# Gate and up projections by Strassen's seven block products in place of eight, with weight sums from accumulating transfers

## The chip, the cores and the metric

The kernel runs on one core of one Trainium2 chip. The metric is the device time of one execution in microseconds, lower is better. The engines named below are PE (TensorE, the matrix engine; PEld is its loading of stationary operands), DVE (VectorE), ACT (ScalarE), POOL (GpSimd) and SP (SyncE, which here only starts transfers).

## The reference

One decoder layer on 512 tokens of width 1024 in float32: a SwiGLU feed-forward layer (FFN1), two causal token mixers side by side, a second SwiGLU layer (FFN2), and a last norm. The change touches the two feed-forward layers only (D_FF is 2816).

```python
def rmsnorm(x, g):
    xf = x.astype(f32)
    y = xf * lax.rsqrt(jnp.mean(xf * xf, axis=-1, keepdims=True) + EPS)
    return (y * g.astype(f32)).astype(x.dtype)

def swiglu(x, w_gate, w_up, w_down):
    return (jax.nn.silu(x @ w_gate) * (x @ w_up)) @ w_down
...
    x = x + 0.5 * swiglu(rmsnorm(x, norm_ffn1), ffn1_gate, ffn1_up, ffn1_down)
    h = rmsnorm(x, norm_mix)
...
    x = x + 0.5 * swiglu(rmsnorm(x, norm_ffn2), ffn2_gate, ffn2_up, ffn2_down)
    return x
```

## The kernel before

Everything is kept transposed: features on the 128 partitions, the 512 tokens along the free dimension. X holds the residual stream as eight tiles of 128x512. Each fp32 product is made of three fast ones (`mac`): an operand is split into a high part, rounded to the fast type, and a low part, the rest, and PE computes high·high, high·low and low·high. So every operand needs a cast on ACT (the high part) and a subtraction on DVE (the low part).

The weights come in an order written out in the list `stream`. `fetch` starts the transfer of a tile of 128x1024 (512 KB) from SP into one of three `raw` buffers, `split` makes the parts `whi` (ACT, L192) and `wlo` (DVE, L193), two buffers each, and `weights` hands a tile out and sees to it that the next one is split and the ones behind it are under way.

A feed-forward layer is `ffn(i, tail)`, with i = 0 for FFN1 and i = 2 for FFN2. For each of 22 column tiles m of the hidden layer it makes the gate and the up product, each over 8 tiles of the contraction: 48 matmuls of 128x512. The norm's factor per token is not applied to the input but behind the product: XN holds X times the gain, split in two, and `factors` computes the row R (tile `rrow`) from the sum of squares. That row is there only behind tile m = 1 (`mean` L257, the square root on ACT and the reciprocal on DVE, L241). `act` (L292 to L301) multiplies both products by R, takes silu, multiplies, and splits the result into `ah` and `al`. In FFN1 the first two column tiles are made in `first_tiles` (L281), in the order in which x arrives. Then come the eight down tiles, one after the other: 22 hidden tiles of three matmuls each, with three chunks of weights per tile (8, 8 and 6 hidden tiles). The very last down tile goes in halves of 256 columns (`last_tile`, L366 and around), so that the last norm can start.

PE's order is that of the program as written. On DVE, ACT, SP and POOL a scheduler sets the order when the program is built; an engine then works through its own list in that order, and waits at the head of it.

Of the kernel before, what the change touches and what calls it, by code (L numbers as in the profile page):

```python
# [58 lines left out]


# [37 lines left out]
def decoder_layer(ctx: ExitStack, tc: tile.TileContext, xT, gains, gus, gu1, dn1, wqk, wv, wvd, wg, wup, wout, gu2, dn2, base, out):  # L98
# [186 lines left out]

    def ffn(i, tail):
        with tc.tile_pool(name=f"ff{i}", bufs=1) as apool:
            A = []
            R = None

            def act(m, ps):
                g = tpool.tile([P, S], F32, name="fg", tag="fg")  # L292
                nc.vector.tensor_tensor(g, ps[0], R, ALU.mult)  # L293
                u = tpool.tile([P, S], F32, name="fu", tag="fu")
                nc.vector.tensor_tensor(u, ps[1], R, ALU.mult)  # L295
                nc.scalar.activation(g, g, AF.Silu)
                nc.vector.tensor_tensor(u, g, u, ALU.mult)
                ah = apool.tile([P, S], F32R, name=f"ah{m}", tag=f"ah{m}")
                al = apool.tile([P, S], F32R, name=f"al{m}", tag=f"al{m}")
                nc.scalar.copy(ah, u)  # L300
                nc.vector.tensor_tensor(al, u, f32(ah), ALU.subtract)  # L301
                A.append((ah, al))

            first = first_tiles() if i == 0 else None
            for m in range(FT):
                if i == 0 and m < 2:
                    ps = first[2 * m:2 * m + 2]
                else:
                    ps = []
                    for j in range(2):  # L310
                        w = weights(i, "gu", 2 * m + j)
                        ps.append(bank("all"))
                        for k in range(KT):
                            mac(ps[j], cols(w, k), XN[k], k == 0, k == KT - 1)
                if m == 0:
                    waits = ps
                    continue
                if m == 1:
                    R = factors(i, bank("all"))
                    act(0, waits)  # L320
# [607 lines left out]
```

## Time and profile before

| | |
|---|---|
| three runs | 1132.74, 1133.61 and 1134.06 us, median 1133.61 |
| the profiled execution | 1133.02 us; its span from first to last instruction 1131.1 us |
| instructions | 13533 |
| PE busy | 99% of the span |
| DVE busy | 53% |
| ACT busy | 37% |
| POOL busy | 2% |

The profiled execution is 0.6 us below the median of the runs, and 1.9 us of it lie around the span. Shares are averages over the whole program; stages differ. A line of a group gives the engine, the operation, what is written and read, its count, the busy time in us, the mean of one in ns, and behind that the idle time ahead of these instructions and what ended it.

### The profile page before, as it was taken

Reading aid. Unit: us, or ns where it says so; the run is one execution under the profiler, and the core shown is the slowest. Engines: PE = TensorE matmul, PEld = TensorE weight load, DVE = VectorE, ACT = ScalarE, POOL = GpSimd, SP = SyncE. Lnnn points to the kernel's source line nnn. Section 1 sums busy time; section 2 is a strip of 40 time slices with the busy share of each in tenths; the row PEclk is TensorE's granted clock in tenths of the full one; section 3 lists DMA queues with packets and bytes.
Section 4 is the critical chain, followed back from the end, with each engine's and each line's share of the span. In section 5 each row is a group of like instructions: output and inputs, shape, how many; then the busy total and the mean of one; then the engine's idle time right before and its main releaser. Section 6 shows DMA issues by size and latency. Waiting matters only on the chain.

```text
span 1131.1 us, 13533 instructions
## 1 busy us (share of the span) xinstructions
PE 1119.1 (99%) x5332; PEld 939.4 (83%) x5332; DVE 600.8 (53%) x968; ACT 413.7 (37%) x637; POOL 20.0 (2%) x34
## 2 busy tenths in 40 slices
PE   9999999999999999999999999999999999999997
PEld 7888888888888888889898888888888888888886
DVE  6744444443333667676877668655644444433323
ACT  5433223322222344444554454443322333222321
POOL 0000000000000100000000000000000000000001
PEclk9999999999999999999999999999999999999999
DMA  6222332233333564445443213322223222233321
GB/s 224 94 94 93 94 110 94 94 89 102 101 88 108 165 191 122 135 134 153 123 133 118 76 61 107 112 93 94 93 93 108 97 93 93 94 103 92 95 84 75
DMA packets 37711, 122.14 MB, mean 108 GB/s; under 512 B 4880, under 2 KB 4880, under 8 KB 37648
## 3 DMA queue, kind: packets, MB, share of 16 engines
q1 hardware_dynamic: 37072, 120.08, 34.4%
q10 hardware_dynamic: 576, 1.20, 0.3%
q8 instruction: 42, 0.69, 0.3%
q14 instruction: 21, 0.17, 0.0%
HBM read 103.44 MB, written 2.10 MB: 93 GB/s over the span
## 4 chain that ended last, share of the span: by engine, by line
PE 96%; DVE 2%; DMA 1%; issue 0%; ACT 0%; SPq 0%; DVEq 0%; ACTq 0%
PE ps_all L210 21%; PE ps_all L209 21%; PE ps_all L211 21%; PE ps_acc L209 8%; PE ps_acc L211 8%; PE ps_acc L210 8%; PE ps_all L281 2%; PE ps_out L681 2%; PE ps_att L662 1%; PE ps_att L210 1%; PE ps_att L209 1%; PE ps_att L211 1%; PE ps_att L637 1%; DMA ks<-qkhl 1%; PE ps_all L422 0%
## 5 line engine op out<-in xcount | busy, mean ns | idle before, releaser
L192 ACT CAST whi<-raw 128x1024 fp32r<-128x1024 f32 (+2 forms) x201 | 203.3, 1013 | 545.1 <-PE ps_all L210 249.8
L193 DVE TENSOR_TENSOR wlo<-raw,whi 128x1024 fp32r<-128x1024 f32 (+2 forms) x202 | 236.3, 1171 | 163.3 <-ACT whi L192 163.2
L209 PE MATMUL ps_all<-xh,whi 128*128 128x512 f32 x672 | 261.4, 389 | 0.0
L210 PE MATMUL ps_all<-xl,whi 128*128 128x512 f32 x672 | 261.4, 389 | 0.0
L211 PE MATMUL ps_all<-xh,wlo 128*128 128x512 f32 x672 | 261.4, 389 | 0.0
L209 PEld LDWEIGHTS ps_all<-xh,whi 128*128 128x128 f32 x672 | 126.1, 188 | 26.4
L210 PEld LDWEIGHTS ps_all<-xl,whi 128*128 128x128 f32 x672 | 126.1, 188 | 26.1
L211 PEld LDWEIGHTS ps_all<-xh,wlo 128*128 128x128 f32 x672 | 126.1, 188 | 26.1
L209 PE MATMUL ps_all<-ah,whi 128*128 128x512 f32 (+1 forms) x374 | 141.2, 377 | 0.0
L211 PE MATMUL ps_all<-ah,wlo 128*128 128x512 f32 (+1 forms) x374 | 140.8, 377 | 0.0
L210 PE MATMUL ps_all<-al,whi 128*128 128x512 f32 (+1 forms) x374 | 140.8, 376 | 0.0
L209 PE MATMUL ps_acc<-xh,whi 128*128 128x512 f32 x304 | 123.2, 405 | 0.0
L211 PE MATMUL ps_acc<-xh,wlo 128*128 128x512 f32 x304 | 118.9, 391 | 0.0
L210 PE MATMUL ps_acc<-xl,whi 128*128 128x512 f32 x304 | 118.9, 391 | 0.0
L295 DVE TENSOR_TENSOR fu<-ps_all,rrow 128x512 f32<-128x512 f32 x44 | 30.4, 691 | 124.1 <-PE ps_all L211 124.0
L211 PEld LDWEIGHTS ps_all<-ah,wlo 128*128 128x128 f32 x374 | 70.4, 188 | 13.0
L209 PEld LDWEIGHTS ps_all<-ah,whi 128*128 128x128 f32 x374 | 70.4, 188 | 13.0
L210 PEld LDWEIGHTS ps_all<-al,whi 128*128 128x128 f32 x374 | 70.4, 188 | 12.8
L293 DVE TENSOR_TENSOR fg<-ps_all,rrow 128x512 f32<-128x512 f32 x44 | 30.4, 691 | 79.4 <-PE ps_all L211 79.3
L211 PEld LDWEIGHTS ps_acc<-xh,wlo 128*128 128x128 f32 x304 | 57.1, 188 | 12.7
L210 PEld LDWEIGHTS ps_acc<-xl,whi 128*128 128x128 f32 x304 | 57.4, 189 | 8.2
L209 PEld LDWEIGHTS ps_acc<-xh,whi 128*128 128x128 f32 x304 | 57.2, 188 | 8.3
(169 smaller groups left out, 1183.9 us busy)
## 6 DMA issues: line engine op xcount, KB each, us to landing
raw<-in_gu_dram SPq DMA_DIRECT2D x84, 512.0 KB, 3.4
raw<-in_dn_dram SPq DMA_DIRECT2D x32, 512.0 KB, 3.5
raw<-in_wqk_dram SPq DMA_DIRECT2D x20, 512.0 KB, 3.5
ks<-qkhl SPq DMA_DIRECT2D x40, 256.0 KB, 4.7
raw<-in_wg_dram SPq DMA_DIRECT2D x16, 512.0 KB, 3.5
raw<-in_dn_dram SPq DMA_DIRECT2D x16, 384.0 KB, 3.1
qs<-qkhl SPq DMA_DIRECT2D x40, 128.0 KB, 2.4
raw<-in_wout_dram SPq DMA_DIRECT2D x8, 512.0 KB, 3.4
```

The source lines that it names most:

```text
L192: nc.scalar.copy(hi[:, s], raw[:, s])
L193: nc.vector.tensor_tensor(lo[:, s], raw[:, s], f32(hi[:, s]), ALU.subtract)
L209: nc.tensor.matmul(ps, wh, xh, start=first, stop=False)
L210: nc.tensor.matmul(ps, wh, xl, start=False, stop=False)
L211: nc.tensor.matmul(ps, wl, xh, start=False, stop=last)
L281: nc.tensor.matmul(ps[j], w[:, at:at + P], x, start=k == 0 and n == 0, stop=k == KT - 1 and n == 2)
L293: nc.vector.tensor_tensor(g, ps[0], R, ALU.mult)
L295: nc.vector.tensor_tensor(u, ps[1], R, ALU.mult)
L637: nc.tensor.matmul(ps[:, :n], Q[NA + h][:, i * P:(i + 1) * P], K[NA + h][:, part, :n], start=part == 0, stop=part == 1)
L662: nc.tensor.transpose(pt[:, n * P:(n + 1) * P], block, ident)
L681: nc.tensor.matmul(to(po), V[v], x[:, first:first + n], start=done == 1, stop=done == 2 * n_products)
```

## The change

From column tile m = PLAIN on (4 in FFN1, 3 in FFN2) a gate and up pair is computed as a product of two-by-two blocks: contraction halves by output halves (gate, up) on the weights' side, contraction halves by token halves on the input's side, with seven products instead of eight. These are 18 + 19 = 37 tiles, below called fast tiles. In each, `fast` makes seven products of 4 contraction tiles and three matmuls of 128x256, that is 84 matmuls of 128x256 where 48 of 128x512 were.

The blocks that are sums are made as follows. On the input's side, `forms` makes four sums of blocks of X times the gain for each of the four k, with ACT and four DVE operations of 256 columns, and splits them (`fh`, `fl`, 128x1024). It needs XN no more than X, but comes behind `factors` and `act` of the tiles 0 and 1. On the weights' side, x is loaded by SP, and a second transfer from POOL adds another block onto its upper half (`fetch_x`, an accumulating transfer of 256 KB); y is loaded and added onto likewise (`fetch_y`); z is loaded plainly (`fetch_z`); two further sums are made on DVE (raw_y, L386, and raw_w, L394). `split_x`, `split_y`, `split_z` and `split_w` make the high and low parts: 3.5 tiles of 128x1024 in place of two. The seven products are put together by the DVE operations on `once`, `both` and `blocks`; R is applied once (to the gate), and the up product's factor R is applied behind the down product (`close`), where a multiplication is added.

The hidden tiles are now kept unsplit (`RAW`), and are split in the down stage by `halved`: eight of them at its start, the others as they come to be used. The down tiles 0 and 1 are made together, hidden tile by hidden tile, and the order of the weights' stream follows.

```diff
+PLAIN = {0: 4, 2: 3}
...
     def down_tiles(i, dn):
-        return [((i, "d", m, c), dn[m][:, cut]) for m in range(KT) for c, cut in enumerate(CHUNKS)]
+        order = [(m, c) for c in range(len(CHUNKS)) for m in (0, 1)] + [(m, c) for m in range(2, KT) for c in range(len(CHUNKS))]
+        return [((i, "d", m, c), dn[m][:, CHUNKS[c]]) for m, c in order]
...
+    def parts_of(raw, hi, lo):
+        nc.scalar.copy(hi, raw)
+        nc.vector.tensor_tensor(lo, raw, f32(hi), ALU.subtract)
+        return hi, lo
...
+    def forms(i, pool):
+        out = []
+        for k in range(KT // 2):
+            y = tpool.tile([P, 2, HALF], F32, name="gx", tag="fu")
+            f = pool.tile([P, 4, HALF], F32, name="form", tag="blocks")
+            g, g2, ng2 = (x[:, n:n + 1] for x, n in ((g_sb, i * KT + k), (g_sb, i * KT + k + 4), (ng, i * KT + k + 4)))
+            nc.scalar.mul(y[:, 0], X[k][:, HALF:], g)
+            nc.scalar.mul(y[:, 1], X[k + 4][:, HALF:], g2)
+            nc.vector.scalar_tensor_tensor(f[:, 0], X[k][:, :HALF], g, y[:, 0], ALU.mult, ALU.subtract)
+            nc.vector.scalar_tensor_tensor(f[:, 1], f[:, 0], -1.0, y[:, 1], ALU.mult, ALU.subtract)
+            nc.vector.tensor_tensor(f[:, 2], y[:, 1], y[:, 0], ALU.subtract)
+            nc.vector.scalar_tensor_tensor(f[:, 3], X[k + 4][:, :HALF], ng2, f[:, 1], ALU.mult, ALU.subtract)
+            out.append(parts_of(f, *(pool.tile([P, 4, HALF], F32R, name=f"f{x}{k}", tag=f"f{x}{k}") for x in "hl")))
+        return out
...
+            def halved(pool):
+                k = len(A)
+                hi = pool.tile([P, S], F32R, name=f"ah{k}", tag=f"ah{k}")
+                A[k] = parts_of(RAW[k], hi, apool.tile([P, S], F32R, name=f"al{k}", tag=f"a{k - 1}"))
+            RAW = {}
+            with tc.tile_pool(name=f"gu{i}", bufs=1) as gpool:
+                gate_up(i, lambda m: RAW.setdefault(m, apool.tile([P, S], F32, name=f"a{m}", tag=f"a{m}")), gpool)
+                halved(apool)
+            with tc.tile_pool(name=f"dn{i}", bufs=1) as dpool:
+                while len(A) < 8:
+                    halved(dpool)
+                down(i, A, lambda: halved(dpool), tail)
...
+        def fetch_x(m):
+            if m < FT:
+                raw["x", m] = t = wpool.tile([P, 1024], F32, tag="raw", name="raw_x", bufs=3)
+                nc.sync.dma_start(t, gx[m - plain])
+                nc.gpsimd.dma_start(t[:, 512:], gx[m - plain][:, :512], accum_op=ALU.add)
...
+        def fetch_y(m):
+            if m < FT:
+                raw["y", m] = t = pool.tile([P, 1024], F32, tag="raw_y", name="raw_y", bufs=2)
+                nc.sync.dma_start(t[:, :512], gx[m - plain][:, 512:])
+                nc.gpsimd.dma_start(t[:, :512], gz[m - plain][:, 512:], accum_op=ALU.add)
...
+        def fetch_z(m):
+            if m < FT:
+                raw["z", m] = t = wpool.tile([P, 1024], F32, tag="raw", name="raw_z", bufs=3)
+                nc.sync.dma_start(t, gz[m - plain])
...
+        def split_x(m):
+            if m < FT:
+                W["x", m] = parts_of(raw["x", m], *(wpool.tile([P, 1024], F32R, tag=f"w{n}", name=f"x{n}", bufs=2) for n in ("hi", "lo")))
...
+        def split_y(m):
+            if m < FT:
+                x, y = raw["x", m], raw["y", m]
+                nc.vector.tensor_tensor(y[:, 512:], y[:, :512], x[:, :512], ALU.add)
+                W["y", m] = parts_of(y, *(pool.tile([P, 1024], F32R, tag=f"y{n}", name=f"y{n}") for n in ("hi", "lo")))
+                fetch_z(m + 1)
+        def split_z(m):
+            if m < FT:
+                y, z = raw["y", m], raw["z", m]
+                w = pool.tile([P, 512], F32, tag="raw_w", name="raw_w")
+                nc.vector.tensor_tensor(w, y[:, 512:], z[:, :512], ALU.add)
+                raw["w", m] = w
+                W["z", m] = parts_of(z, *(pool.tile([P, 1024], F32R, tag=f"z{n}", name=f"z{n}") for n in ("hi", "lo")))
+                fetch_y(m + 2)
+                fetch_x(m + 2)
+        def split_w(m):
+            if m < FT:
+                W["w", m] = parts_of(raw["w", m], *(pool.tile([P, 512], F32R, tag=f"w{n}", name=f"w{n}") for n in ("hi", "lo")))
+        def product(ps, w, at, x, first=False, last=False):
+            for k in range(4):
+                wh, wl = (v[:, at + k * P:at + (k + 1) * P] for v in w)
+                xh, xl = x(k)
+                nc.tensor.matmul(ps, wh, xh, start=first and k == 0, stop=False)
+                nc.tensor.matmul(ps, wh, xl, start=False, stop=False)
+                nc.tensor.matmul(ps, wl, xh, start=False, stop=last and k == 3)
...
+        def fast(m):
+            x, y, z = (W.pop((n, m)) for n in "xyz")
+            b1, b2, b3, b4 = (bank("all").rearrange("p (c n) -> p c n", c=2) for _ in range(4))
+            c = pool.tile([P, 4, HALF], F32, name="blocks", tag="blocks")
+            t = tpool.tile([P, 2, HALF], F32, name="both", tag="fu")
+            product(b1[:, 0], x, 0, block(0, 0), first=True, last=True)
+            product(b2[:, 1], x, 512, form(2), first=True)
+            split_x(m + 1)
+            product(b2[:, 0], y, 0, form(0), last=True)
+            product(b3[:, 1], y, 512, form(1), first=True)
+            split_y(m + 1)
+            product(b3[:, 0], z, 0, block(1, 0), last=True)
+            once = pool.tile([P, HALF], F32, name="once", tag="once")
+            nc.scalar.copy(once, b1[:, 0])
+            nc.vector.tensor_tensor(c[:, 0::3], twice(once), b3, ALU.add)
+            u = c[:, 3]
+            nc.vector.tensor_tensor(t, twice(u), b2, ALU.add)
+            nc.vector.tensor_tensor(c[:, 3], t[:, 0], b2[:, 1], ALU.add)
+            product(b4[:, 1], z, 512, form(3), first=True)
+            split_z(m + 1)
+            product(b4[:, 0], W.pop(("w", m)), 0, block(1, 1), last=True)
+            split_w(m + 1)
+            nc.vector.tensor_tensor(c[:, 1:3], t, b4, ALU.add)
+            g = tpool.tile([P, S], F32, name="fg", tag="fg")
+            flat = c.rearrange("p c n -> p (c n)")
+            nc.vector.tensor_tensor(g, flat[:, :S], R, ALU.mult)
+            nc.scalar.activation(g, g, AF.Silu)
+            nc.vector.tensor_tensor(hidden(m), g, flat[:, S:], ALU.mult)
...
+        def begin(at):
+            if at == 1:
+                fetch_x(plain)
+                fetch_y(plain)
+            elif at == 2:
+                fetch_z(plain)
+                fetch_y(plain + 1)
+            elif at == 3:
+                fetch_x(plain + 1)
+                split_x(plain)
+                split_y(plain)
+                split_z(plain)
+                split_w(plain)
...
+                RS[i] = R = factors(i, bank("all"))
+                act(0, waits)
+                act(1, ps)
+                F = forms(i, pool)
+            else:
                 act(m, ps)
-            for m in range(KT - (i == 2)):
-                ps = bank("all")
-                for c in range(len(CHUNKS)):
-                    w = weights(i, "d", m, c)
-                    for k in range(8 * c, min(8 * c + 8, FT)):
-                        mac(ps, cols(w, k - 8 * c), A[k], k == 0, k == FT - 1)
-                nc.vector.scalar_tensor_tensor(X[m], ps, 0.5, X[m], ALU.mult, ALU.add)
-                tail(m)
-            if i == 2:
-                last_tile(A)
+        for m in range(plain, FT):
+            fast(m)
+    def down(i, A, halved, tail):
+        def close(m, ps):
+            t = tpool.tile([P, S], F32, name="fd", tag="fg")
+            nc.vector.tensor_tensor(t, ps, RS[i], ALU.mult)
+            nc.vector.scalar_tensor_tensor(X[m], t, -0.5, X[m], ALU.mult, ALU.add)
+            tail(m)
+        ps = [bank("all"), bank("all")]
+        for c in range(len(CHUNKS)):
+            ws = [weights(i, "d", 0, c), weights(i, "d", 1, c, ahead=2)]
+            for k in range(8 * c, min(8 * c + 8, FT)):
+                if len(A) < FT:
+                    halved()
+                for m in range(2):
+                    mac(ps[m], cols(ws[m], k - 8 * c), A[k], k == 0, k == FT - 1)
+        for m in range(2):
+            close(m, ps[m])
+        for m in range(2, KT - (i == 2)):
+            ps = bank("all")
+            for c in range(len(CHUNKS)):
+                w = weights(i, "d", m, c)
+                for k in range(8 * c, min(8 * c + 8, FT)):
+                    mac(ps, cols(w, k - 8 * c), A[k], k == 0, k == FT - 1)
+            close(m, ps)
```

How the lists of the engines change is shown at three places. The first is DVE at the start of FFN2, from `mean` (the first operation that needs the sum of squares) on. Before, these are the rows from there:

```order
L257 TENSOR_SCALAR mean<-ps_all_6408 128x512
L193 TENSOR_TENSOR wlo<-raw,whi 128x1024
L241 RECIPROCAL root<-root 128x512
L242 SCALAR_TENSOR_TENSOR step<-root 128x512
L243 TENSOR_TENSOR step<-step,mean 128x512
L193 TENSOR_TENSOR wlo<-raw,whi 128x1024
L244 SCALAR_TENSOR_TENSOR rrow<-step,root 128x512
L293 TENSOR_TENSOR fg<-ps_all_6290,rrow 128x512
```

With the change 40 rows stand from `mean` up to the last form's low part: the one reciprocal, 8 operations of 128x1024, 15 of 128x512 and 16 of 128x256. (At the start of FFN1 they are 47: one reciprocal, 11, 19 and 16.) The last twelve of the 40, with `fl` the low parts of the forms for k = 1, 2 and 3:

```order
L221 TENSOR_TENSOR fl_7615<-form,fh_7614 128x1024
L313 SCALAR_TENSOR_TENSOR form<-x_91,g_sb,gx 128x256
L315 TENSOR_TENSOR form<-gx 128x256
L314 SCALAR_TENSOR_TENSOR form<-form,gx 128x256
L316 SCALAR_TENSOR_TENSOR form<-x_95,ng,form 128x256
L221 TENSOR_TENSOR fl_7627<-form,fh_7626 128x1024
L313 SCALAR_TENSOR_TENSOR form<-x_92,g_sb,gx 128x256
L315 TENSOR_TENSOR form<-gx 128x256
L314 SCALAR_TENSOR_TENSOR form<-form,gx 128x256
L316 SCALAR_TENSOR_TENSOR form<-x_96,ng,form 128x256
L221 TENSOR_TENSOR fl_7639<-form,fh_7638 128x1024
L221 TENSOR_TENSOR xlo<-raw_x,xhi 128x1024
```

So the factor's chain, the first fast tile's weights and all forms stand in one list, and `form` has one buffer: the next k is built only when the low part of the one ahead has been taken. The first fast tile's second product on PE reads all four.

The second place is DVE in the middle of the gate and up stage. Before, a column tile had these rows (gate weights, up weights, `act`):

```order
L293 TENSOR_TENSOR fg<-ps_all_504,rrow 128x512
L193 TENSOR_TENSOR wlo<-raw,whi 128x1024
L295 TENSOR_TENSOR fu<-ps_all_535,rrow 128x512
L297 TENSOR_TENSOR fu<-fg,fu 128x512
L193 TENSOR_TENSOR wlo<-raw,whi 128x1024
L301 TENSOR_TENSOR al_567<-fu,ah_566 128x512
```

Now a fast tile has these twelve (low parts of z, w, x and y, the sums of weights, the putting together of the products, and the hidden tile `a`):

```order
L439 TENSOR_TENSOR blocks<-once,ps_all_7866 128x2x256
L441 TENSOR_TENSOR both<-blocks,ps_all_7865 128x512
L221 TENSOR_TENSOR zlo<-raw_z,zhi 128x1024
L442 TENSOR_TENSOR blocks<-both,ps_all_7865 128x256
L447 TENSOR_TENSOR blocks<-both,ps_all_7867 128x512
L221 TENSOR_TENSOR wlo<-raw_w,whi 128x512
L450 TENSOR_TENSOR fg<-blocks,rrow 128x512
L394 TENSOR_TENSOR raw_w<-raw_y,raw_z 128x512
L386 TENSOR_TENSOR raw_y<-raw_y,raw_x 128x512
L221 TENSOR_TENSOR xlo<-raw_x,xhi 128x1024
L452 TENSOR_TENSOR a_7990<-fg,blocks 128x512
L221 TENSOR_TENSOR ylo<-raw_y,yhi 128x1024
```

Six rows have become twelve: three of 1024 columns, eight of 512 and one of 256. On SP and POOL the load of the next tile's `raw_x` waits for this tile's `xlo`, since raw_x goes round through a single one of the three `raw` buffers, and POOL's accumulating transfer waits for that load.

The third place is PE at the start of the down stage of FFN1, where `ah` and `al` are the parts of a hidden tile. Before, one down tile ran alone:

```order
L209 MATMUL ps_all_1794<-ah_998,whi 128x512
L210 MATMUL ps_all_1794<-al_999,whi 128x512
L211 MATMUL ps_all_1794<-ah_998,wlo 128x512
L209 MATMUL ps_all_1794<-ah_1070,whi 128x512
L210 MATMUL ps_all_1794<-al_1071,whi 128x512
L211 MATMUL ps_all_1794<-ah_1070,wlo 128x512
```

Now two run together, with one chunk of weights each:

```order
L227 MATMUL ps_all_2872<-ah_2836,whi 128x512
L228 MATMUL ps_all_2872<-al_2837,whi 128x512
L229 MATMUL ps_all_2872<-ah_2836,wlo 128x512
L227 MATMUL ps_all_2873<-ah_2836,whi 128x512
L228 MATMUL ps_all_2873<-al_2837,whi 128x512
L229 MATMUL ps_all_2873<-ah_2836,wlo 128x512
```

Both `whi` and both `wlo` buffers are in use up to the last hidden tile of a chunk pair.

## Rows read from the trace of the kernel before

**Rows 1.** The page: span, and each engine's busy time, share and count

```profile
span 1131.1 us, 13533 instructions
PE 1119.1 (99%) x5332; PEld 939.4 (83%) x5332; DVE 600.8 (53%) x968; ACT 413.7 (37%) x637; POOL 20.0 (2%) x34
```

**Rows 2.** The page: the chain that ended last, by engine

```profile
PE 96%; DVE 2%; DMA 1%; issue 0%; ACT 0%; SPq 0%; DVEq 0%; ACTq 0%
```

**Rows 3.** Windows: stretch, then PE, PEld, DVE, ACT, POOL, granted clock, DMA share, GB/s

```profile
28.70:245.80 217.10, 217.10 (x959) 179.77 (x958) 109.29 (x130) 69.98 (x86) 0.00 (x0) 1.00 0.30 96
246.10:365.50 119.40, 119.40 (x528) 98.89 (x527) 42.27 (x47) 32.25 (x39) 0.00 (x0) 1.00 0.32 95
757.10:996.60 239.50, 239.50 (x1058) 198.31 (x1057) 116.81 (x138) 76.14 (x93) 0.00 (x0) 1.00 0.30 96
```

**Rows 4.** Timeline of PE, gate and up: 63 matmuls of 512 columns, first and last

```profile
199.63 0.39 PE L211 MATMUL ps_all<-xh,wlo 128*128 128x512 f32 x1
...
213.69 0.39 PE L210 MATMUL ps_all<-xl,whi 128*128 128x512 f32 x1
```

**Rows 5.** Timeline of PE, last down tile: 26 matmuls of 256 columns, first and last

```profile
1115.34 0.28 PE L210 MATMUL ps_all<-al,whi 128*128 128x256 f32 x1
...
1118.33 0.28 PE L211 MATMUL ps_all<-ah,wlo 128*128 128x256 f32 x1
```

**Rows 6.** Groups on DVE by form

```profile
L193 DVE TENSOR_TENSOR wlo<-raw,whi 128x1024 fp32r<-128x1024 f32 x170 | 208.1, 1224 | 112.1 <-ACT whi L192 112.0
L293 DVE TENSOR_TENSOR fg<-ps_all,rrow 128x512 f32<-128x512 f32 x44 | 30.4, 691 | 79.4 <-PE ps_all L211 79.3
L241 DVE RECIPROCAL root<-root 128x512 f32<-128x512 f32 x3 | 10.1, 3354 | 3.3 <-ACT root L240 3.3
L378 DVE TENSOR_TENSOR yo<-yo,ps_all 128x256 f32<-128x256 f32 x6 | 2.2, 416 | 1.2 <-ACT rrow L368 1.2
```

**Rows 7.** Timeline of DVE, operations back to back

```profile
675.23 3.10 DVE L800 TENSOR_TENSOR yl<-y,yh 128x512 fp32r<-128x512 f32 x5
786.62 1.22 DVE L193 TENSOR_TENSOR wlo<-raw,whi 128x1024 fp32r<-128x1024 f32 x1
787.75 0.68 DVE L244 SCALAR_TENSOR_TENSOR rrow<-step,root 128x512 f32<-128x512 f32 x1
1125.42 1.75 DVE L378 TENSOR_TENSOR yo<-yo,ps_all 128x256 f32<-128x256 f32 x5 [1.20 <-ACT rrow L368]
```

**Rows 8.** Groups on ACT by form

```profile
L192 ACT CAST whi<-raw 128x1024 fp32r<-128x1024 f32 x170 | 179.2, 1054 | 484.9 <-PE ps_all L210 243.6 <-issue 193.9 <-PE ps_acc L210 27.8
L296 ACT ACTIVATE fg<-fg 128x512 f32<-128x512 f32 x44 | 27.6, 628 | 6.6 <-DVE fg L293 6.5
```

**Rows 9.** Timeline of DVE at the start of FFN1 and of FFN2

```profile
28.70 0.69 DVE L257 TENSOR_SCALAR mean<-ps_all 128x512 f32<-128x512 f32 x1 [3.54 <-PE ps_all L253]
...
31.28 3.35 DVE L241 RECIPROCAL root<-root 128x512 f32<-128x512 f32 x1 [0.72 <-ACT root L240]
...
779.53 0.69 DVE L257 TENSOR_SCALAR mean<-ps_all 128x512 f32<-128x512 f32 x1 [3.81 <-PE ps_all L253]
...
781.89 3.35 DVE L241 RECIPROCAL root<-root 128x512 f32<-128x512 f32 x1 [0.53 <-ACT root L240]
```

**Rows 10.** The chain that ended last, in order of time: start, us, what

```profile
28.66 0.23 PE ps_all L209
```

**Rows 11.** Timeline of PE, matmuls behind the factors of FFN2

```profile
779.11 0.39 PE L253 MATMUL ps_all<-sl,ones_r 128*128 128x512 f32 x1
779.33 0.39 PE L209 MATMUL ps_all<-xh,whi 128*128 128x512 f32 x1
```

**Rows 12.** Timeline of PE, the first matmuls of the program

```profile
1.45 4.64 PE L422 MATMUL ps_all<-wide 128*128 128x512 f32 x10 [1.45 <-DVE wide L128]
```

**Rows 13.** DMA issues: what, queue, count, size, median us to landing

```profile
raw<-in_gu_dram SPq DMA_DIRECT2D x84, 512.0 KB, 3.4
ks<-qkhl SPq DMA_DIRECT2D x40, 256.0 KB, 4.7
x<-in_xT_dram SPq DMA_DIRECT2D x8, 256.0 KB, 5.4
out_dram<-yo SPq DMA_DIRECT2D x8, 256.0 KB, 2.2
```

**Rows 14.** Timeline of DVE, close of the last down tile

```profile
1119.44 0.42 DVE L348 SCALAR_TENSOR_TENSOR x<-ps_all,x 128x256 f32<-128x256 f32 x1 [2.42 <-PE ps_all L211]
```

More of the change, by code (lines that the diff above doesn't have):

```diff
@@ L97, in decoder_layer @@
 @with_exitstack
-def decoder_layer(ctx: ExitStack, tc: tile.TileContext, xT, gains, gus, gu1, dn1, wqk, wv, wvd, wg, wup, wout, gu2, dn2, base, out):
+def decoder_layer(ctx: ExitStack, tc: tile.TileContext, xT, gains, gus, gu1, gx1, gz1, dn1, wqk, wv, wvd, wg, wup, wout, gu2, gx2, gz2, dn2, base, out):
     nc = tc.nc
@@ L126, in decoder_layer @@
     g_sb = cpool.tile([P, 4 * KT], F32, name="g_sb")
+    ng = cpool.tile([P, 3 * KT], F32, name="ng")
     wide = tpool.tile([P, S], F32R, name="wide", tag="fg")
@@ L138, in decoder_layer @@
     nvs = [cpool.tile([P, 4, 2], F32, name=f"nv{h}") for h in range(2)]
-    cpool.tile([P, 40], F32, name="round")
+    cpool.tile([P, 16], F32, name="round")
     CHUNKS = [slice(c * P, min(c + 8, FT) * P) for c in range(0, FT, 8)]
@@ L157, in decoder_layer @@
     stream += [(("out", m), wout[m]) for m in range(KT)]
-    stream += [((2, "gu", t), gu2[t]) for t in range(2 * FT)]
+    stream += [((2, "gu", t), gu2[t]) for t in range(2 * PLAIN[2])]
+    fences.append(len(stream))
     stream += down_tiles(2, dn2)
@@ L195, in split, with weights @@
             state["split"] += 1
-    def weights(*key):
+    def weights(*key, ahead=3):
         t = state["at"]
@@ L201, in weights @@
         state["at"] += 1
-        split(t + 1)
-        fetch(t + 3)
+        end = (fences + [len(stream)])[0] - 1
+        split(min(t + 1, end))
+        fetch(min(t + ahead, end))
         return splits.pop(t)
+    def parts_of(raw, hi, lo):
+        nc.scalar.copy(hi, raw)
+        nc.vector.tensor_tensor(lo, raw, f32(hi), ALU.subtract)
+        return hi, lo
     def mac(ps, w, x, first, last):
@@ L286, in ffn @@
+    RS = {}
     def ffn(i, tail):
         with tc.tile_pool(name=f"ff{i}", bufs=1) as apool:
[L288 to L314, printed above, removed]
-                if m == 0:
[L316 to L320, printed above, removed]
-                act(m, ps)
@@ new lines, in ffn @@
+            apool.tile([P, S], F32R, name="al_room", tag="a-1")
+            def halved(pool):
[6 more added lines that the diff above has]
+                halved(apool)
@@ L366, in write @@
             nc.tensor.matmul(pr[h], ones, diag.rearrange("p t q -> p (t q)"), start=True, stop=True)
-            row = tpool.tile([P, HALF], F32, name="rrow", tag=("rrow", "ssq")[h], bufs=1)
+            row = xpool.tile([P, S], F32, name=f"last{h}", tag=f"xl{h}")[:, :HALF]
             nc.scalar.copy(row, pr[h])
@@ L900, in pairs_of, with blocks @@
         return np.ascontiguousarray(np.stack([x, y], 1).reshape(-1, P, x.shape[-1]))
-    gu1 = pairs_of(a["ffn1_gate"][0], a["ffn1_up"][0])
+    gu1, gu2 = (pairs_of(a[f"ffn{n}_gate"][0], a[f"ffn{n}_up"][0]) for n in (1, 2))
+    def blocks(gu, plain):
+        gate, up = gu[2 * plain::2], gu[2 * plain + 1::2]
+        return [np.ascontiguousarray(np.concatenate([gate[:, :, s], up[:, :, s]], 2)) for s in (slice(0, 512), slice(512, 1024))]
+    (gx1, gz1), (gx2, gz2) = blocks(gu1, PLAIN[0]), blocks(gu2, PLAIN[2])
     arrays = {
@@ L915 @@
         "wout": _tiles(a["w_out"][0]),
[L916 removed]
+        "gu2": gu2[:2 * PLAIN[2]],
+        "gx2": gx2,
+        "gz2": gz2,
         "dn2": _tiles(a["ffn2_down"][0]),
```

58 lines of the change are left out of this document (54 added, 4 removed).

## The prediction, before the changed kernel ran

> **What bounds the kernel now.** I read the page first: PE is busy for 1119.1 of 1131.1 us, DVE for 53%, ACT for 37% [rows 1]. Then the chain that ended last: 96% of it is PE [rows 2]. PE waits almost nowhere, so each microsecond of matmuls saved is a microsecond of the program, as long as no other engine makes PE wait. Then the windows of the stages: in gate and up (28.7 to 245.8 us in FFN1, 757.1 to 996.6 us in FFN2) PE is busy throughout at a granted clock of 1.00, the 2.4 GHz level, while DVE is busy for 109 of 217 and 117 of 240 us; in the down stage for 42 of 119 us [rows 3]. There is half an engine of room on DVE in gate and up. Last the timelines, for the pace of matmuls back to back: 62 steps of 512 columns in 14.06 us, 0.2268 us each [rows 4], and 25 steps of 256 columns in 2.99 us, 0.1196 us each [rows 5]. So half the columns cost 0.53 of the time, with as many loads of weights as before, which therefore do not bound at this size.
>
> **The gain.** A column tile costs 48 x 0.2268 = 10.89 us now, a fast one 84 x 0.1196 = 10.05 us. That is 0.84 us a tile, and 37 tiles give **-31.0 us**. Of the eighth that the block form saves in products, 0.53 in place of 0.50 takes half away.
>
> **The middle of the stage.** DVE has a longer list. Its pace in a row is less than the mean of a group: five operations of 512 columns in 3.10 us, so 0.61 each; 1.13 us from one of 1024 to the next operation; 0.35 each for five of 256 [rows 7] (the groups' means are 1.22, 0.69 and 0.42 [rows 6], since the ends overlap). A fast tile's twelve rows cost 3 x 1.13 + 8 x 0.61 + 0.35 = 8.6 us of PE's 10.05: tight, but it fits; by the means of the groups it would be 9.6, and fits too. ACT has three and a half casts of 1024 (1.05 each), a silu of 0.63 and a copy [rows 8], below 5 us. The transfers carry 1792 KB a tile in place of 1024, so their share rises from 0.30 [rows 3] to about 0.55 by estimate. I put the middle of the stage at nothing beyond PE's 10.05, with one doubt, the accumulating transfer (below).
>
> **The start of the fast tiles** is where I see the loss. PE's second product needs the forms of all four k, and DVE's list puts the factors' chain, the first fast tile's weights and the four forms into one row behind `mean`.
> FFN2: `mean` starts at 779.53 [rows 9]. The 40 rows up to the last form's low part cost 3.35 (the reciprocal) + 8 x 1.13 + 15 x 0.61 + 16 x 0.34 = 27.0 us, so DVE cannot be through before 806.5. It also waits: 0.53 us for the root before the reciprocal [rows 9], and twice (k = 2 and 3) for ACT's cast of a whole form, 1.05 us and the signals around it, since `form` has one buffer; walked row by row with smaller waits I come to 810.0. PE leaves the factors at 779.33 [rows 11], makes one plain tile (10.89), the first product (12 x 0.1196 = 1.43) and three quarters of the second (1.2), and wants the last form at 792.8. **+17.2 us**, and 13.7 if DVE never waited.
> FFN1: `mean` at 28.70 [rows 9], 47 rows with 3.35 + 11 x 1.13 + 19 x 0.61 + 16 x 0.34 = 32.8 us, so 61.5 at the earliest and 65.0 by the walk. PE is at its third column tile at 28.66 [rows 10], makes two plain ones (21.8) and wants the last form at 53.0. **+12.0 us**, at least 8.5.
> What covers the forms is one plain tile in FFN2 and two in FFN1; what is left open is DVE's list.
>
> **The clock behind these stalls.** PE is nearly idle for 12 and 17 us there. No row shows PE restarting from such a gap within the program; the nearest is the program's start, where ten matmuls of 512 columns took 4.64 us right after idling [rows 12], 0.46 each, the pace of the lower level of 1.2 GHz and slower, though the granted clock is given as whole there. 4.64 - 10 x 0.2268 = 2.4 us lost. At each of two starts that is **+4.7 us**, between nothing (the pace stays) and twice that.
>
> **The down stages.** Three things, by the same prices. At the start the second hidden tile's parts stand on ACT behind the last fast tile's sums, silu and product (0.61 + 0.61 + 0.63 us and a further one), then 0.63 for the cast and 0.61 for the low part, about 3.4 us behind the last matmul, where PE has 6 x 0.2268 = 1.4 us of the first: 2.0 us. At the change of a chunk, both buffers of `whi` and `wlo` are held until the end of the pair, so the next cast (1.05) and subtraction (1.13) start only 0.7 us before PE is through: about 1.6 and 1.0 us at the two changes, 2.05 at the passage to tile 2. Together 6.65 us, in both layers **+13.3**. Lower bound 4 (the hidden tiles' waits alone), upper 16 (each change in full). The multiplication added to each `close` is off PE's path but in the last tile: **+0.4**, by an operation of 256 columns such as the one at 1119.44 [rows 14]. Behind FFN1's last tile it is 0 to 0.6; I take 0, since PE's chain before has no wait on DVE there.
>
> **Sum** from the profiled execution, 1133.0 us, which lies 0.6 below the median: -31.0 + 12.0 + 17.2 + 4.7 + 13.3 + 0.4 = +16.6, so **1150 us**.
>
> **The accumulating transfer.** No row has one. The next load of raw_x waits for this tile's `xlo`, so one turn is: load 3.4 us [rows 13], accumulate T, cast 1.05, low part 1.22, and 0.3 of signals, 6.0 + T. It stays below 10.05 as long as T is below 4.05. Bounds for T by the rows of 256 KB: 2.2 us for a plain store, 4.7 from SBUF to SBUF, 5.4 for the loads of x at the start [rows 13]. A read, an addition and a write lies nearer to the SBUF row than to the plain store; I take 4, just under the limit.
> The Trainium skill ("DMA: Bandwidth & Descriptors", "Anatomy of one DMA — SWDGE (gpsimd) path") gives transfers started by GpSimd as 2.0 us plus the bytes at 436 GB/s; its estimate for 256 KB is 2.6 us, by which the turn would be 8.6 us and this term nothing. It says nothing of what the addition costs, and no run here shows one yet.
>
> **The rivals.**
> 1. *The accumulating transfer binds.* Each turn beyond 10.05 is paid 18 or 19 times a layer, less some 4.8 us by which x is ahead at first. At T = 4.7: 0.65 x 18 - 4.8 and 0.65 x 19 - 4.8, +14 in all; at 5.4, 1.35 us a turn, +40. So 1164 to 1190. For it: one buffer, and T bounded only from 2.2 to 5.4. Against it: the queues are half empty.
> The Trainium skill ("SBUF — State Buffer", "Who interferes with whom") tells of transfers from GpSimd that starve while VectorE runs certain copies in a two-port mode, but that `tensor_tensor` was not seen to do so; nearly all of DVE's operations here are of that kind, so by that rule T would not be lengthened by DVE. No run here shows it yet.
> 2. *The starts cost only DVE's bare work and the changes in the down stage are mostly covered* (the other side): 8.5 + 13.7 for the starts, no loss of clock, 4 for the down stages: 1133.0 - 31.0 + 22.2 + 4 + 0.4 = 1129. It turns to faster once all stalls stay below 31 us. For it: the walk's waits are mine, and ACT is at 37%. Against it: two of the waits for casts stand in the list itself.
> 3. *The forms are hidden after all* (PE finds them ready): only down costs remain, 1133.0 - 31.0 + 4 to 13 = 1106 to 1115. Against it: DVE's bare work is too long for it.
> 4. *The pace of 256 columns is not that of rows 5*: were a matmul bound by the load of weights alone, 939.4 / 5332 = 0.176 us [rows 1], a fast tile would take 14.8 us, +145. Rows 5 speak against it, with the same kind of loads.
>
> **How the numbers follow.** My forecast, 1138 to 1162 us: 0.45. Rival 1: 0.23. Rival 2, 1122 to 1135: 0.22. Rival 3: 0.07. The rest: 0.03. The range from 1122 to 1180 leaves out rival 3, the upper third of rival 1 and the rest, some 0.17. A difference of 0.2%, 2.3 us, is about what a measurement of this kernel tells from none. Faster: rival 3 and 0.19 of rival 2, 0.26. Same: 0.05. Slower: 0.69.
>
> **What would show it.** In the profile of the changed kernel, PE should idle about 12 us around 53 us and 17 us around 793 us in the old time, ended by the low part of a form; matmuls of 256 columns should follow each other every 0.12 us in the fast tiles; DVE should be busy for 85 to 95% of that stretch; at the starts of the down stages there should be gaps of 1 to 2 us ended by `al` or `wlo`. I am wrong if the forms are ready when PE comes (then rival 3), or if each fast tile has a gap on xhi or xlo (then rival 1).

## The result

The changed kernel takes 1263.86 us, median of four runs (1263.08 to 1265.59), against 1133.41 us before: 1.1153 times the time, with a 95% interval from 1.1134 to 1.1172. I had forecast 1150 us, with 1122 to 1180 as the range. Slower was right, but three quarters of the loss (97.6 of 130.5 us) were not where I saw it.

The page of the changed kernel: the span, each engine's busy time, and the chain that ended last by engine [rows 1, 2].

```profile
span 1262.4 us, 17168 instructions
PE 1152.0 (91%) x6664; PEld 1018.9 (81%) x6664; DVE 789.1 (63%) x1278; ACT 490.0 (39%) x772; POOL 84.2 (7%) x108
...
PE 54%; DVE 10%; DMA 6%; issue 3%; ACT 1%; SPq 0%; DVEq 0%; ACTq 0%; POOLq 0%
```

PE is no longer the whole chain: 54% of it against 96%, with DVE and transfers in between. Where, the windows tell (columns as in [rows 3]): in order the start of the fast tiles in FFN1, their middle, the down stage, and the same three of FFN2.

```profile
50.30:72.00 21.70, 6.73 (x29) 5.01 (x28) 12.91 (x21) 6.12 (x8) 0.86 (x1) 0.64 0.34 83
72.00:293.60 221.60, 198.20 (x1485) 193.93 (x1484) 149.47 (x205) 75.32 (x103) 25.88 (x30) 0.92 0.57 136
293.70:427.50 133.80, 126.85 (x529) 101.39 (x529) 59.33 (x74) 42.56 (x59) 0.00 (x0) 0.96 0.28 81
...
852.40:875.00 22.60, 7.54 (x30) 5.56 (x30) 18.37 (x31) 12.42 (x18) 0.86 (x1) 0.63 0.25 60
875.00:1110.90 235.90, 206.94 (x1568) 202.05 (x1567) 158.37 (x217) 79.43 (x109) 27.64 (x32) 0.93 0.56 136
1111.00:1241.00 130.00, 122.64 (x552) 99.60 (x552) 53.46 (x66) 42.72 (x65) 0.00 (x0) 0.96 0.24 70
```

The starts look as forecast in kind: PE stands nearly still there. The middle does not: PE is busy for 198 of 222 us there, at a granted clock of 0.92, and DVE, which I had feared to be full, for 149. FFN1's gate and up takes 265.2 us (28.5 to 293.7) in place of 217.6, FFN2's 291.7 (819.3 to 1111.0) in place of 239.8, and each down stage 14 to 15 us more; the mixers between are unchanged.

The waits of the changed kernel (what waited for what: us in total, times, longest) give the middle's pattern:

```profile
ACT xhi L220 <- DMA raw_x<-in_gx_dram: 215.9, 30, 8.3
...
DVE raw_y L386 <- DMA raw_y<-in_gz_dram: 135.5, 31, 5.4
...
PE ps_all L416 <- DVE ylo L221: 40.2, 26, 2.8
...
PE ps_all L414 <- ACT fh L220: 20.3, 6, 8.3
```

One fast tile in the timelines of the changed kernel (SP, POOL, ACT, then DVE):

```profile
142.37 0.33 SPq L354 DMA_DIRECT2D raw_x<-in_gx_dram  x1
144.10 0.33 SPq L362 DMA_DIRECT2D raw_y<-in_gx_dram  x1
...
146.46 0.86 POOL L355 DMA_DIRECT2D raw_x<-in_gx_dram  x1 [10.22 <-DMA raw_x<-in_gx_dram]
147.85 0.86 POOL L363 DMA_DIRECT2D raw_y<-in_gz_dram  x1 [0.54 <-DVE blocks L447]
...
152.46 1.05 ACT L220 CAST xhi<-raw_x 128x1024 fp32r<-128x1024 f32 x1 [7.30 <-DMA raw_x<-in_gx_dram]
...
142.86 1.22 DVE L221 TENSOR_TENSOR ylo<-raw_y,yhi 128x1024 fp32r<-128x1024 f32 x1
...
153.70 0.69 DVE L386 TENSOR_TENSOR raw_y<-raw_y,raw_x 128x512 f32<-128x512 f32 x1 [4.43 <-DMA raw_y<-in_gz_dram]
154.31 1.22 DVE L221 TENSOR_TENSOR xlo<-raw_x,xhi 128x1024 fp32r<-128x1024 f32 x1
155.44 0.69 DVE L452 TENSOR_TENSOR a<-fg,blocks 128x512 f32<-128x512 f32 x1
156.05 1.22 DVE L221 TENSOR_TENSOR ylo<-raw_y,yhi 128x1024 fp32r<-128x1024 f32 x1
```

Read it as a ring. `ylo` ends at 144.08 and frees a buffer; at 144.10 SP loads the y of two tiles on into it; POOL adds the second block from 147.85; at 153.70 L386 can sum; then xlo, a, and the next `ylo` at 156.05, which PE waits for. From `ylo` to `ylo` 13.19 us. raw_y has two buffers, but in DVE's list the sum of the next tile's y stands ahead of this tile's `ylo`, so the second buffer buys nothing. A second ring runs beside it: xlo ends, x is loaded (142.37), added onto (146.46), cast (152.46), xlo. Each holds one accumulating transfer, which from issue to landing took 5.5 and 5.6 us (DMA issues of the changed kernel):

```profile
raw_y<-in_gz_dram POOLq DMA_DIRECT2D x37, 256.0 KB, 5.5
raw_x<-in_gx_dram POOLq DMA_DIRECT2D x37, 256.0 KB, 5.6
```

### The profile page after: what moved, and what is told of

It reads as the page before. It is cut to its first block, busy times and chain, and to the rows that moved or that the text cites. A ratio compares the mean times of both kernels' runs of the same rounds, so it can differ in the third digit from the quotient of the medians.

```text
span 1262.4 us, 17168 instructions
## 1 busy us (share of the span) xinstructions
PE 1152.0 (91%) x6664; PEld 1018.9 (81%) x6664; DVE 789.1 (63%) x1278; ACT 490.0 (39%) x772; POOL 84.2 (7%) x108
## 3 DMA queue, kind: packets, MB, share of 16 engines
q0 software_dynamic: 10656, 19.40, 9.1%
## 4 chain that ended last, share of the span: by engine, by line
PE 54%; DVE 10%; DMA 6%; issue 3%; ACT 1%; SPq 0%; DVEq 0%; ACTq 0%; POOLq 0%
PE ps_acc L227 7%; PE ps_acc L229 7%; PE ps_acc L228 7%; PE ps_all L229 7%; PE ps_all L227 6%; PE ps_all L228 6%; DMA raw_y<-in_gz_dram 5%; PE ps_all L416 2%; PE ps_all L415 2%; PE ps_all L414 2%; DVE xlo L221 2%; PE ps_out L877 2%; PE ps_att L858 1%; PE ps_att L227 1%; PE ps_att L228 1%
## 5 line engine op out<-in xcount | busy, mean ns | idle before, releaser
L204 ACT CAST whi<-raw 128x1024 fp32r<-128x1024 f32 (+2 forms) x127 | 124.2, 986 | 277.6 <-PE ps_all L228 139.0
L205 DVE TENSOR_TENSOR wlo<-raw,whi 128x1024 fp32r<-128x1024 f32 (+2 forms) x128 | 145.6, 1141 | 134.0 <-ACT whi L204 114.1
L416 PE MATMUL ps_all<-fh,ylo 128*128 128x256 f32 x296 | 99.3, 336 | 40.2 <-DVE ylo L221 40.2
L220 ACT CAST xhi<-raw_x 128x1024 fp32r<-128x1024 f32 x37 | 38.8, 1047 | 227.2 <-DMA raw_x<-in_gx_dram 215.9
L386 DVE TENSOR_TENSOR raw_y<-raw_y,raw_x 128x512 f32<-128x512 f32 x37 | 25.6, 692 | 139.1 <-DMA raw_y<-in_gz_dram 135.5
L414 PE MATMUL ps_all<-fh,yhi 128*128 128x256 f32 x296 | 97.0, 328 | 12.2 <-ACT yhi L220 12.0
L416 PEld LDWEIGHTS ps_all<-fh,ylo 128*128 128x128 f32 x296 | 69.2, 234 | 45.9 <-DVE ylo L221 45.9
L415 PE MATMUL ps_all<-fl,yhi 128*128 128x256 f32 x296 | 95.1, 321 | 0.0
L414 PEld LDWEIGHTS ps_all<-fh,yhi 128*128 128x128 f32 x296 | 68.5, 231 | 15.6 <-ACT yhi L220 15.6
L415 PEld LDWEIGHTS ps_all<-fl,yhi 128*128 128x128 f32 x296 | 68.6, 232 | 0.0
L414 PE MATMUL ps_all<-fh,xhi 128*128 128x256 f32 x148 | 44.0, 297 | 25.3 <-ACT fh L220 20.3
```

Source lines behind the costliest of these rows:

```text
L204: nc.scalar.copy(hi[:, s], raw[:, s])
L205: nc.vector.tensor_tensor(lo[:, s], raw[:, s], f32(hi[:, s]), ALU.subtract)
L220: nc.scalar.copy(hi, raw)
L386: nc.vector.tensor_tensor(y[:, 512:], y[:, :512], x[:, :512], ALU.add)
L414: nc.tensor.matmul(ps, wh, xh, start=first and k == 0, stop=False)
L415: nc.tensor.matmul(ps, wh, xl, start=False, stop=False)
```

## The experiments

The kernel before took 1132.9 to 1133.2 us beside these runs. Where no interval or median is given, a time is a single run; the five repeats of one kernel at the end lie within 0.6%. The interval between two fast tiles, in brackets, is that between two loads of y from SP, median between 100 and 250 us, the middle of FFN1's stage; in the changed kernel it is 13.4 us.

**The transfers taken out.** Theory A: the rings set the interval. Theory B: DVE's list and PE's pace. Theory C: the bandwidth.

```diff
-                nc.gpsimd.dma_start(t[:, 512:], gx[m - plain][:, :512], accum_op=ALU.add)
...
-                nc.gpsimd.dma_start(t[:, :512], gz[m - plain][:, 512:], accum_op=ALU.add)
```

> Both accumulating transfers are left out (x and y then lack the block that they would add, so two weight blocks are not the sums). Theory A (two turns of transfers: y's and x's, of 13.2 and 12.4 us a fast tile, each holding one accumulating transfer of 5.5 to 6 us): both turns fall below 8 us, the fast tiles come to 10.1 to 10.6 us, and the time to about 1264 - 37 x 2.6 = 1168 us (1155 to 1180). Theory B (DVE's longer list and PE's slow starts make the 12.8 us, the transfers only fill the gaps): above 1235 us. Theory C (the accumulating transfers cost their bandwidth, not their latency: 19.4 MB of 151): some 1240 us.

1166.29 us [10.08], where theory A gave 1168. The loads of x follow each other at PE's own pace, eleven steps in 110.87 us; first and last row of the timeline of SP in this run:

```profile
101.37 0.33 SPq L354 DMA_DIRECT2D raw_x<-in_gx_dram  x1
...
212.24 0.33 SPq L354 DMA_DIRECT2D raw_x<-in_gx_dram  x1
```

Then one ring at a time (the second line of the diff alone, and the first alone):

> Only y's accumulating transfer is left out (y then lacks one block), x's stays. Theory A (y's turn binds at 13.2 us, x's lies right behind it at 12.4): a fast tile takes about 12.4 us, the time falls by 35 x 0.8 = 28 to about 1236 us (1225 to 1245). If x's turn alone binds, as my prediction's rival had it: no more than 5 us gained, above 1258. If only y's turn counts: about 1170.

1218.43 us [12.1], below the 1225 to 1245 that I had expected by theory A: x's ring alone needs 12.1 us, not 12.4.

> Only x's accumulating transfer is left out (x then lacks one block), y's stays: the counterpart of the run without y's. Theory A (y's turn binds at 13.2 us, with POOL's start of y's transfer no longer behind x's): 12.3 to 12.9 us a tile, 1235 to 1255 us. If x's turn alone binds: about 1170 us.

1228.57 us [12.1], a little below what I expected. Each ring alone gives 12.1 us, both together 13.4. POOL's queue does not make the difference: POOL starts y's transfer 3.8 us after y's load with x's transfers in its queue and 3.9 us without them (medians of the same stretch). What differs is the transfer, 5.5 us for y's beside x's and 4.7 us alone. From the DMA issues, y's in the run without x's, then x's in the run without y's:

```profile
raw_y<-in_gz_dram POOLq DMA_DIRECT2D x37, 256.0 KB, 4.7
raw_x<-in_gx_dram POOLq DMA_DIRECT2D x37, 256.0 KB, 5.4
```

Why y's takes longer beside x's is not shown. The ring that I had as a rival, x's, would have been slower than PE by itself.

**More room, all work kept.** First x alone:

```diff
+            raws[t] = wpool.tile([P, 1024], F32, tag=f"raw{t % 3}", name="raw", bufs=1)
...
-                raw["x", m] = t = wpool.tile([P, 1024], F32, tag="raw", name="raw_x", bufs=3)
+                raw["x", m] = t = wpool.tile([P, 1024], F32, tag=f"raw{(m - plain) % 2}", name="raw_x", bufs=1)
...
+                raw["z", m] = t = wpool.tile([P, 1024], F32, tag="raw2", name="raw_z", bufs=1)
```

> All work kept; raw_x has two buffers of its own in turn, raw_z the third, in place of the scheduler's choice among three. Theory A (y's turn binds): x's turn is gone, y's stays, within 12 us of 1264 us. If x's turn alone binds, as my prediction's rival had it: the fast tiles come to 10.1 to 10.6 us, about 1168 us.

1273.94 us [13.3]: y's ring stays, as theory A has it. (This edit leaves z one buffer, and the next run shows that z's ring then takes 12.1 us; so 1168 us could not have come out here whichever ring bound, but 13.3 lies above z's ring too.) Then y's too, by a tile of one buffer for the sum, which forces it behind `ylo`:

```diff
-                nc.vector.tensor_tensor(y[:, 512:], y[:, :512], x[:, :512], ALU.add)
+                raw["v", m] = v = pool.tile([P, 512], F32, tag="raw_v", name="raw_v")
+                nc.vector.tensor_tensor(v, y, x[:, :512], ALU.add)
```

> All work kept; raw_x has two buffers in turn as in the run before, and y's sum on DVE goes into a tile of its own with one buffer, so that it must stand behind the low part of the tile before instead of ahead of it (the cast and the low part of y become two of 512 columns each). Both turns then have two tiles' time. Theory A: fast tiles of 10.1 to 10.7 us, DVE at about 8.9 us a tile, time about 1168 us (1155 to 1185). Theory B or C (DVE's amount of work, or the bandwidth): no gain, above 1235 us.

1227.53 us [12.1], ratio 1.0834 (1.0802 to 1.0865). My expectation failed: I had given z only one buffer and so made a third ring. Its waits say so:

```profile
DVE raw_w L397 <- DMA raw_z<-in_gz_dram: 104.3, 33, 4.7
ACT zhi L220 <- DMA raw_z<-in_gz_dram: 81.8, 29, 6.2
```

With a second buffer for z, in the room that y's sum had freed:

```diff
+                raw["z", m] = t = (pool if (m - plain) % 2 else wpool).tile([P, 1024], F32, tag=("raw2", "raw_z")[(m - plain) % 2], name="raw_z", bufs=1)
```

> All work kept; as the run before (y's sum in a tile of one buffer, raw_x two buffers in turn), and raw_z gets a second buffer as well, in the room that y's sum freed. In the run before, raw_z with one buffer made a new turn of 12 us (load 6 us, sum, low parts of y, low part of z). Theory A (the tile lasts as long as the longest turn of a buffer): no turn is left above 10 us, fast tiles of 10.1 to 10.5 us, time about 1168 us (1158 to 1180), as without the accumulating transfers at all. Theory B (DVE's work or the transfers' bandwidth bounds): as the run before, 1220 to 1230 us.

1166.49 us [10.08], the same as without the transfers. So every accumulating transfer is there, with its bytes and its latency (6.6 us for y's and 5.1 for x's in this run's DMA issues), DVE and ACT have even one more operation each a tile, and nothing is paid: theories B and C fall.

**What makes the transfer long.**

```diff
-                nc.gpsimd.dma_start(t[:, 512:], gx[m - plain][:, :512], accum_op=ALU.add)
+                nc.gpsimd.dma_start(t[:, 512:], gx[m - plain][:, :512])
...
-                nc.gpsimd.dma_start(t[:, :512], gz[m - plain][:, 512:], accum_op=ALU.add)
+                nc.sync.dma_start(t[:, :512], gz[m - plain][:, 512:])
```

> The addition is left out of both second transfers, with the bytes and places kept: x's is a plain transfer from POOL, y's a plain one from SP (so x and y hold a copied block in place of a sum). It prices the accumulating transfer's 5.5 us from issue to landing. If the addition (read, add, write) costs the time, x's plain one from POOL lands in about 2.5 to 3.5 us. If it is the way through POOL's queue, x's still lands in about 5 us, and y's from SP in 2.2 to 3.3 us. The time lies between 1166 us (no second transfers) and 1264 us: about 1190 by the first, 1210 by the second, since x's turn of 12.4 then falls only in the first.

1195.9 us [11.2]. Its DMA issues:

```profile
raw_y<-in_gz_dram SPq DMA_DIRECT2D x37, 256.0 KB, 3.2
raw_x<-in_gx_dram POOLq DMA_DIRECT2D x37, 256.0 KB, 2.9
```

The same 256 KB from the same POOL land in 2.9 us without the addition and in 5.6 with it. POOL's queue is emptier here, since y's transfer has left it; but in the run without y's it held x's transfers alone as well, and with the addition they took 5.4 us. The queue is not the price, the addition is.

The run shows a second thing. With two copies, of 2.9 and 3.2 us, the tile still takes 11.2 us and the program 29.6 us more than without the transfers, and it is `ylo` that PE waits for in this run:

```profile
PE ps_all L416 <- DVE ylo L221: 17.4, 19, 2.0
```

So the ring through y is too long even where nothing is added.

**The starts.**

```diff
-PLAIN = {0: 4, 2: 3}
+PLAIN = {0: 6, 2: 6}
```

> As the run before, with six plain column tiles in both layers in place of 4 and 3 (32 fast tiles in place of 37). My prediction's step on the starts: PE waits some 15 and 18 us there for the last form, and the pace after it is slow. If the forms are what is waited for, 2 and 3 more plain tiles (21.8 and 32.7 us) cover them: minus 33 to 40 for the stalls and the pace behind them, plus 5 x 0.84 = 4 for the gain given up: about 1168 - 33 = 1135 us (1128 to 1142). If the stalls at the start are not the forms but the first weights of the fast tiles, they move along: 1165 to 1175.

1134.39 us: 32.1 us less, and with the 4.2 us of gain given up the starts had cost 36 in the version with two buffers each. PE waits for no form there.

**The down stage.**

```diff
+            if key[:1] in ((0,), (2,)) and key[1:3] == ("d", 1):
+                hi, lo = (SIDE[0].tile([P, 1024], F32R, tag=f"side{n}", name=f"w{n}", bufs=2) for n in ("hi", "lo"))
...
-            ws = [weights(i, "d", 0, c), weights(i, "d", 1, c, ahead=2)]
+            ws = [weights(i, "d", 0, c), weights(i, "d", 1, c, on=2)]
```

(`on` says how many tiles ahead the parts are made.)

> As the run before, and in the down stage the parts of tile 1's weights get buffers of their own (two of hi and lo), so that the next chunk's parts are made while this one is used. My prediction put 6.65 us of waits on each down stage, the trace has 6.9 us of waits and some 7 more by a slow pace behind them. If the chunk changes cause 4.4 of the waits and the pace falls with each of them: minus 2 x (4.4 + 4) = 17 us, 1135 - 17 = 1118 us (1110 to 1126), which would be faster than the kernel before. If the pace does not hang on these waits: minus 9, 1126 us.

1132.29 us (0.9994, 0.9984 to 1.0003): next to nothing, and my expectation of 1118 failed. The changes of a chunk had no wait left, but tile 1's first parts now lay in memory that comes free only with the last fast tile, and their casts came behind others. The timeline of ACT:

```profile
236.64 3.73 ACT L225 CAST ah<-a 128x512 fp32r<-128x512 f32 x7 [0.80 <-DVE a L461]
240.28 1.99 ACT L209 CAST whi<-raw 128x1024 fp32r<-128x1024 f32 x2
```

PE stood still from 234.4 to 241.4 us. With the extra buffers for the second chunk instead:

```diff
+            if key[1] == "d" and key[2:] in ((0, 1), (1, 1), (2, 0)):
...
+            ws = [weights(i, "d", 0, c, on=1 + (c == 1)), weights(i, "d", 1, c, on=2 - (c == 2))]
```

> Six plain tiles and two buffers each as before; in the run before this, PE had no wait at the chunk changes, but waited 7.4 us at the start of each down stage, since tile 1's first parts lay in memory that comes free with the last fast tile, behind eight casts on ACT. Here the first chunk's parts of both tiles lie in the old two buffers, and those of the second chunk (and of tile 2's first) in two further ones. If the chunk changes are what the down stage loses beside its start: about 2.5 us of wait and 4 us of slow pace stay at each start, 2 x (4.4 of waits + 2 of pace) are gone against the version with six plain tiles alone (1134.4), 1122 us (1117 to 1128). If the slow pace comes at the start of the stage whatever the waits: 1128 to 1132 us.

1119.24 us, 15.2 less than with six plain tiles alone. FFN1's down stage takes 124.4 us there, 4.7 more than in the kernel before; in the changed kernel it was 14.3 more. Timed again, with five plain tiles in FFN2 in one run and as it was in another:

> As the run beside it with five plain tiles in the second layer in place of six: 2 x 10.88 us still cover the 18 us of the last form there, one more tile gains 0.84 us: 1121 us, or 0.984 to 0.994 of the kernel before. If five do not cover: 1124 us or more.

1125.48 us, 0.9932 (0.9918 to 0.9945): five do not cover, PE waited once for 3.4 us for a form and ran slowly behind it.

> The kernel of the single run e9 once more, unchanged, timed in five rounds against the kernel before: 1119 us (1118 to 1122), ratio 0.986 to 0.990, so faster than both. If the single run was a lucky one: 1122 to 1126, as with five plain tiles in the second layer.

1118.39 us, median of five (1116.1 to 1122.77), 0.9878 of the kernel before (0.9858 to 0.9898): 1.2% faster than that, and faster than with five plain tiles. PE's waits that are left in it:

```profile
PE ps_all L232 <- ACT ah L225: 4.5, 2, 2.3
PE ps_all L556 <- ACT sql L552: 2.3, 1, 2.3
```

## Why the prediction was wrong

**The gain was right.** Fast tiles follow each other every 10.08 us where nothing holds them; the sum had 10.05. Against 10.89 for a plain tile the 37 tiles give 30 us.

**The accumulating transfer is the step that failed, twice over.** The sum put the middle of the stage at nothing beyond PE's pace, because the turn through raw_x "stays below 10.05 as long as T is below 4.05", and "I take 4, just under the limit".

First, T was too small: it was 5.5 to 5.6 us, above even the upper bound that I had drawn from loads [rows 13]. None of those rows is a transfer that adds, so 5.4 us was no upper bound for one. The Trainium skill's fit ("DMA: Bandwidth & Descriptors", "Anatomy of one DMA — SWDGE (gpsimd) path") gave 2.6 us; the plain transfer from POOL took 2.9, so for that it about agrees, and of the addition it says nothing. The Trainium skill's rule on starving ("SBUF — State Buffer", "Who interferes with whom") has nothing against it here: 2.9 us beside a DVE busy with `tensor_tensor`.

Second, the limit was that of the wrong ring. I had followed the buffer of raw_x, which is one, and passed over raw_y, since it has two. The rows of DVE's order that I had printed show L386 in front of xlo, a and ylo; I read them as work to be added up, not as a list in which one operation that waits holds up those behind it. By the pieces of the trace (medians of the same stretch), `ylo` 1.2 us, 3.8 from the load to POOL's start, and 2.4 from the sum to the next `ylo`, the ring through y is 7.4 + T. It passes 10.05 once T is above 2.6 or so. A T of 4, had it been right, would not have saved the forecast: with copies of 2.9 and 3.2 us the time was 1195.9 us, above my range already.

My rival 1 had the right kind of mechanism, a transfer in a ring of a buffer, at a chance of 0.23, but the wrong ring: PE's gaps in the fast tiles were to be on xhi or xlo, and they are on `ylo` and yhi. With T at 5.5 its turn of 6.0 + T would have come to 11.5 us and some 1194 us; x's ring alone measured 12.1 us and 1218, both rings 1264. The transfers in their rings cost 1263.9 - 1166.3 = 97.6 us, and I had put them at nothing.

**The starts: the mechanism was right, FFN1's size was not.** PE waits for the last form as said, and behind it runs at the lower level. Timeline of PE, first and last of six such waits in FFN1, and windows behind the last one:

```profile
60.56 0.58 PE L414 MATMUL ps_all<-fh,xhi 128*128 128x256 f32 x1 [8.27 <-ACT fh L220]
...
70.60 0.58 PE L415 MATMUL ps_all<-fl,xhi 128*128 128x256 f32 x1 [0.68 <-DVE fl L221]
```

```profile
70.60:76.70 6.10, 6.10 (x28) 6.10 (x29) 1.23 (x1) 1.41 (x2) 0.00 (x0) 0.50 0.25 86
76.90:80.00 3.10, 3.10 (x29) 3.10 (x28) 2.51 (x3) 1.03 (x2) 0.86 (x1) 1.00 0.33 22
```

The six waits make 15.0 us where I had 12.0, and the last form came at 70.6, not 65.0. Most of the missing 5.6 us is the transfers again: DVE's list stood still for 4.97 us for a cast that waited for x, ahead of the second form's low part (ACT, then DVE):

```profile
57.21 1.04 ACT L220 CAST xhi<-raw_x 128x1024 fp32r<-128x1024 f32 x1 [7.42 <-DMA raw_x<-in_gx_dram]
58.29 1.23 DVE L221 TENSOR_TENSOR xlo<-raw_x,xhi 128x1024 fp32r<-128x1024 f32 x1 [4.97 <-ACT xhi L220]
```

Without the accumulating transfers the same matmul came within 0.7 us of my 65.0:

```profile
65.64 0.58 PE L413 MATMUL ps_all<-fl,xhi 128*128 128x256 f32 x1 [0.68 <-DVE fl L221]
```

A clock of 0.50 is the level of 1.2 GHz, and 28 matmuls in 6.10 us lose 2.7 us against 0.1196 each; I had 2.4. Both starts together: 29.2 + 4.7 = 33.9 forecast, 36 measured by the run with six plain tiles, where no ring binds.

**The down stages: the waits were right, their consequence was left out.** FFN1's waits, from the timeline of PE:

```profile
297.56 0.50 PE L227 MATMUL ps_all<-ah,whi 128*128 128x512 f32 x1 [2.26 <-ACT ah L220]
298.29 0.53 PE L228 MATMUL ps_all<-al,whi 128*128 128x512 f32 x1 [0.23 <-DVE al L221]
309.71 0.50 PE L227 MATMUL ps_all<-ah,whi 128*128 128x512 f32 x1 [0.24 <-ACT whi L204]
312.52 0.80 PE L229 MATMUL ps_all<-ah,wlo 128*128 128x512 f32 x1 [2.07 <-DVE wlo L205]
327.57 0.50 PE L229 MATMUL ps_all<-ah,wlo 128*128 128x512 f32 x1 [0.26 <-DVE wlo L205]
335.99 0.50 PE L227 MATMUL ps_all<-ah,whi 128*128 128x512 f32 x1 [0.24 <-ACT whi L204]
338.27 0.50 PE L229 MATMUL ps_all<-ah,wlo 128*128 128x512 f32 x1 [1.55 <-DVE wlo L205]
```

They make 6.85 us, and I had 6.65. That the sum fits so well is in part luck: at the start, the two changes and the passage to tile 2 they are 2.5, 2.3, 0.3 and 1.8, for 2.0, 1.6, 1.0 and 2.05. The stage became 14.3 us longer all the same: the other half is PE's pace. I had charged the clock only at the long stalls. The end of the program, behind the last product, is off too, by 2.5 us in place of 0.4: there PE waited 2.34 us for the squares, 0.97 before, which is 1.4 of it.

Put together with what was measured, 1133.0 - 30 + 36 + 29 + 2.5 = 1170.5 us, against 1166 us for the two runs that are free of the rings; the rest to 1264 is theirs.

## What to carry to other kernels

A transfer that adds cannot be priced by rows of transfers that copy; where a new latency stands in a ring of a buffer, work out at which latency the ring binds, and if that lies inside the bounds, count it as likely to bind. Two buffers are two only if the engine's list lets them be: find in the order the operation that waits for the new data, and see whether the one that frees the old buffer stands behind it. The block form itself paid once each of its waits had room or cover: 1.2% faster than before, with 32 tiles in place of 37.
